# Half-row matmuls of a two-layer mixer kernel given all 128 rows of TensorE's array, with zeros in the rows that are not theirs

## The chip, the core and the metric

The kernel runs on one core of one Trainium2 chip. The metric is the device time of one execution in microseconds (us), median of several runs. TensorE's array has 128 rows (the contraction dimension) and 128 columns. An operand that lies on 64 partitions uses 64 of the rows, and the profile then writes a matmul as 64\*128. Operands are fp32, or fp32r, a form of fp32 that TensorE takes in one pass; a plain fp32 matmul appears in the trace as two records, one for each pass.

## What is computed

Two layers (DEPTH = 2) over 512 tokens, 256 of context and 256 latent, with 1024 features. A layer is a half-step of SwiGLU feed-forward, a mixer, and a second half-step. The mixer has three branches whose gated outputs are summed. In short, from the reference:

```
q, k = heads of differential attention: 4 heads, 2 maps m of 64 features each
s  = einsum('bqhmd,bkhmd->bhmqk', q, k);  pr = softmax(s)
y  = (pr[:, :, 0] - lam * pr[:, :, 1]) @ v
mLSTM, 4 heads of 64:   s = einsum('bhtd,bhsd->bhts', qb, kb) * exp(dlog - mt)
RWKV-7, per direction:  w_raw = w0[d] + tanh(p[wl]) @ w2[d]     (64 x 512)
                        a     = sigmoid(a0[d] + p[al] @ a2[d])  (64 x 512)
```

All three have a contraction over 64 values: a map of an attention head, an mLSTM head, a direction's low-rank matrix. In the last layer context queries are not needed.

## The kernel before

Every dense product is made exact in fp32 by splitting each operand in a leading part hi and a remainder lo, and adding three fp32r matmuls (hi by hi, hi by lo, lo by hi). A unit is 128 x 1024 weights: SP loads it into `raw`, ScalarE casts it to `hi` (L140), VectorE subtracts to get `lo` (L144), and TensorE runs 24 matmuls of 128\*128 on it (`fm_tile`, or `tm_group` with 256 columns each). These are the rows named d and m. All matmuls go through the helper `mm` (L102), all transposes through `tr` (L105).

Within a mixer, the work of two kinds is mixed. The RWKV-7 branch goes through four tiles t of 128 channels; each has elementwise work with small matmuls (`rwkv_stage1`, `rwkv_stage2`), a triangular solve (`rwkv_solve`: 64 matmuls of 32\*32, sG and sB, behind 31 steps on VectorE) and a chain over eight chunks (`rwkv_chain`: X, U, S, Y, of 64\*64 and 128\*64). It runs under `tc.high_priority()`. Everything else (`mixers`: attention, then mLSTM, then the merge) is a generator that yields after each step with an estimate of its time; the table BUDGET says how much of it is put behind each RWKV-7 tile, and the rest follows at the end. The order on each engine is what the framework's scheduler makes of the program, by priority and by its own costs, so an edit at one place can move instructions elsewhere.

The matmuls that the change touches:

- **Attention scores**, aS. `attn_rot` makes q and k of a head, feature-major, in two tiles qkT [128, 512]: map 0 on partitions 0 to 63, map 1 on 64 to 127. `attn_head` takes the 64 rows of one map for each matmul, fp32.
- **mLSTM scores**, mS. Two heads share a tile mqk, one on each half of the partitions; the head's 64 rows are taken, fp32.
- **Low-rank low parts**, loral. The hi part lorah carries the direction's matrix twice, so that x with hi on one half and lo on the other is a 128-row matmul (lw, la from lorah). The remainder loral [128, 2, 128] is used on the direction's 64 rows only, fp32r.
- **Gate-row transposes**, gT. The mLSTM gates have 64 rows gi and 64 rows Fc; each is transposed in four blocks against a 64 x 64 identity.

The same 64\*128 form remains, untouched, in A (`rwkv_stage2`). 

Of the kernel before, what the change touches and what calls it, by code (L numbers as in the profile page):

```python
# [9 lines left out]
F32 = mybir.dt.float32  # L10
# [25 lines left out]
# columns of the packed per-partition parameters  # L36
# [3 lines left out]
# columns of the packed constants  # L40
# [10 lines left out]
# per layer: gate tiles after each attention and mLSTM head; other work (in us of TensorE) before and after  # L51
# the columns of each next recurrent tile
# [24 lines left out]
SPLIT = 16  # L77

class Halves:
    """a unit's 1024 columns in two tiles"""
# [9 lines left out]
class Builder:  # L92
# [36 lines left out]
    def unit(self, spec):  # L129
        """hi and lo parts of a unit; exact together"""  # L130
# [16 lines left out]
    def unit_early(self, spec):  # L147
        """a unit in room that the feed-forward part doesn't need yet"""
        raw = self.fp.tile([P, 1024], F32, name="araw", tag="araw", bufs=4)
        self.unit_load(raw, spec)  # L150
        r = []
        for i, tag in enumerate(("uh", "ul")):
            r.append(Halves([self.fp.tile([P, 1, NT], F32R, name=tag, tag=tag, bufs=14) for _ in range(2)]))
        for n in range(2):
            c = slice(n * NT, (n + 1) * NT)
            self.split(r[0][:, c], r[1][:, c], raw[:, c])
        return r
# [4 lines left out]
    def fm_tile(self, spec, lo=0, h=None, ps=None):  # L162
        """one feature-major tile of 128 columns: PSUM [128 cols, tokens]"""
        hi, lw = self.unit(spec)
        return self.fm_mm(hi, lw, range(KT), slice(lo, NT), h or self.h, ps=ps)
# [15 lines left out]
    def fm_first(self, units, pss, parts):  # L181
        """the first tiles after a norm: every feature block goes to all of them as soon as it is there"""
# [10 lines left out]
    def split(self, hi, lo, src):  # L193
        """exact split of src: hi carries the leading half of the significand"""
# [3 lines left out]
    def rsqrt(self, out, in_, eps, scale=1.0):  # L198
        """out = 1/sqrt(scale*in + eps)"""
# [8 lines left out]
    def ada_first(self, i, j):  # L208
        """block j of modulation vector i (0 shift, 1 scale) of the first norm, on TensorE"""
# [18 lines left out]
    def ada_first_shift(self, j):  # L228
        """the shift on VectorE"""
# [13 lines left out]
    def load_c(self, after=lambda: None):  # L243
        """silu of the two condition vectors on every partition"""
# [23 lines left out]
    def ada_steps(self):  # L268
        """the others on VectorE: one block of 128 outputs at a time"""
# [27 lines left out]
    def sqrt_ahead(self):  # L297
        """has ScalarE's table for the square roots of the next norm loaded before they are due"""
# [4 lines left out]
    def sumsq(self, k, c):  # L303
        """adds the squares of x_k to the running sum of these tokens"""
# [9 lines left out]
    def norm_stats(self, parts):  # L314
        """1 / rms of these tokens on every partition, in PSUM"""
# [16 lines left out]
    def norm_apply(self, l, i, k, psr, parts):  # L332
        """feature block k of the modulated norm, split into hi and lo"""
# [12 lines left out]
    def norm_mod(self, l, i, parts):  # L346
        """norm and modulation of these tokens"""
# [5 lines left out]
    def x_update(self, l, gi, k, ps, c):  # L353
        """x_k += 0.5 * gate * ps"""
# [12 lines left out]
    def ffn(self, l, which, lo, ready, after):  # L367
        """ready: the PSUM tiles of the first gate and up tiles;
        after: token ranges with what to do when x has its final value there"""
# [60 lines left out]
    def conv(self, out, ps, w, lo=0):  # L430
        """out = centred 3-tap convolution of ps; w: three [128,1] taps"""
# [11 lines left out]
    def attn_prep(self):  # L443
# [21 lines left out]
        self.qg, self.nl, self.subw = qg, nl, sub  # L465

    def tm_group(self, cols, consume, t0=0):
        """token-major product with 256 columns (cols: (c0, width) ranges): PSUM [128 tokens, 256]
        for each of the token tiles from t0 on"""
# [19 lines left out]
    def attn_qk(self, h):  # L489
        """raw q and k of a head, token-major (token tile, q or k), and the sums of their squares"""  # L490
# [14 lines left out]
    def attn_qk_pair(self, hp):  # L505
        """the same for two heads without the context's q: slots k0 k1 q2 k2 q3 k3 of the token tiles"""
# [32 lines left out]
    def attn_rot(self, qkr, ss):  # L539
        """normalised and rotated q and k of a head, feature-major"""  # L540
# [29 lines left out]
        for w in range(2):  # L570
# [4 lines left out]
            o = a.tile([P, NT], F32, name="qkT", tag="qkT", bufs=4)  # L575
            nc.scalar.copy(o[:, t0 * P :], pt[:, t0 * P :])
# [3 lines left out]
    def attn_head(self, hp, h, qT, kT, v):  # L580
# [3 lines left out]
        for i in range(lo // P, 4):  # L584
# [4 lines left out]
            for m in range(2):  # L589
                pS = self.psm("aS")  # L590
                r = slice(64 * m, 64 * m + 64)
                self.mm(pS[:, : nk * P], qT[r, i * P : (i + 1) * P], kT[r, : nk * P], True, True)
# [52 lines left out]
    def mlstm_steps(self):  # L645
# [4 lines left out]
        def qk(c0, ti, lo):  # L650
# [5 lines left out]
            o = a.tile([P, NT], F32, name="mqk", tag="mqk", bufs=4)  # L656
            nc.vector.scalar_tensor_tensor(o[:, lo:], th[:, lo:], 1.0, z[:, lo:], op0=ALU.add, op1=ALU.mult)
            return o

        q, k = [], []  # L660
# [3 lines left out]
        for i in range(2):  # L664
            k.append(qk(O_MK + P * i, 2 + i, 0))
            yield 5
        # gates: rows 0-3 i fwd, 32-35 i bwd, 64-67 f fwd, 96-99 f bwd (others zero)
        pg = self.fm_tile([("w_gate", l, kk * P, 0, P) for kk in range(KT)])
        gb = pv[:, PV_GB : PV_GB + 1]
        gi = a.tile([64, NT], F32, name="gi", tag="P00", bufs=1)  # L670
# [24 lines left out]
        # m = F + G; em = exp(-m); nG = -G, its hi part on the first half of the partitions, lo on the other  # L695
        nc.vector.tensor_tensor(Fc, Fc, G, op=ALU.add)
# [7 lines left out]
        for t in range(4):  # L704
            self.tr(pt[:, t * 64 : t * 64 + 64], gi[:, t * P : (t + 1) * P], 64)
        for t in range(4):
            self.tr(pt[:, 256 + t * 64 : 256 + t * 64 + 64], Fc[:, t * P : (t + 1) * P], 64)
        used = lambda x: x.rearrange("p (t d r) -> p (t d) r", t=4, d=2)[:, :, 0:4]
        nc.scalar.copy(ac.rearrange("p t (d r) -> p (t d) r", d=2), used(pt[:, :256]))
        nc.scalar.activation(em.rearrange("p t (d r) -> p (t d) r", d=2), used(pt[:, 256:]), AF.Exp, scale=-1.0)  # L710
# [5 lines left out]
        for h in range(4):  # L716
            if h % 2 == 0:
# [9 lines left out]
                yield 10  # L727
            ps = self.fm_tile(self.blocks("w_in", l, O_MO + h * P), lo)
            tho = a.tile([P, NT], F32, name="tho", tag="tho", bufs=1)
            nc.scalar.activation(tho[:, lo:], ps[:, lo:], AF.Tanh, scale=0.5)  # L730
            r = slice(64 * (h % 2), 64 * (h % 2) + 64)
            qt, kt = q[h // 2], k[h // 2]
            # s-block j: scores against the query tokens it can reach
# [9 lines left out]
            for j in range(4):  # L743
                s0 = max(lo, 0 if j < 2 else CTX)
                pS = self.psm("mS")
                self.mm(pS[:, s0:], kt[r, j * P : (j + 1) * P], qt[r, s0:], True, True)
                for d in range(2):
                    # reachable query blocks
# [66 lines left out]
    def rwkv_small(self):  # L815
# [6 lines left out]
        # hi and lo parts of a direction on the two halves of the partitions  # L822
# [4 lines left out]
        for src, dst in ((tw, self.tw), (pa, self.ta)):  # L827
            for d in range(2):
                r, o = slice(64 * d, 64 * d + 64), slice(64 - 64 * d, 128 - 64 * d)
                nc.scalar.copy(dst[r, d], src[r])  # L830
                nc.vector.tensor_tensor(dst[o, d], src[r], dst[r, d].bitcast(F32), op=ALU.subtract)
        self.vpad = a.tile([P, 128 + NT], F32, name="vpad", tag="vpad", bufs=1)
# [22 lines left out]
    def rwkv_cols(self, t):  # L855
# [12 lines left out]
        ll = a.tile([P, 2, P], F32R, name="loral", tag="loral", bufs=1)  # L868
        nc.scalar.copy(lh, lw)
        for d in range(2):  # L870
            r = slice(64 * d, 64 * d + 64)
            nc.vector.tensor_tensor(ll[r], lw[r, d::2], lh[r, d::2].bitcast(F32), op=ALU.subtract)
# [9 lines left out]
    def rwkv_stage1(self, t, r, k, v, lw, g2):  # L882
        """everything that is elementwise over (channel, token)"""
# [5 lines left out]
        # normalised keys  # L889
# [5 lines left out]
        # 1 / max(norm, 1e-12)  # L895
# [7 lines left out]
        for d in range(2):  # L903
            rows = slice(64 * d, 64 * d + 64)

            def lora(name, i, x):
                ps = self.pss(name)
                self.mm(ps, lw[0][:, 2 * i + d], x[:, d], True, False)
                self.mm(ps, lw[1][rows, i], x[rows, d], False, True)
# [36 lines left out]
    def rwkv_stage2(self, t, r, k, v, g2, kk, eC, dirs):  # L946
# [6 lines left out]
        # token-major v and the u of each chunk: head 0 has v on partitions 0-63 and u on 64-127,  # L953
        # head 1 the other way round. Token window w is tokens 64w-64 .. 64w+64
# [46 lines left out]
        # bonus  # L1001
# [7 lines left out]
    def rwkv_solve(self, t, Zf):  # L1009
        """Bt[(h, s), (d, c), t] = transpose of (I - A)^-1, A strictly triangular in (t, s)"""  # L1010
        nc, a = self.nc, self.a2
        Bt = self.Bts[t % 2]
        # Zf[(h, s), (d, c), t]: the diagonal blocks first
# [7 lines left out]
        # backward units: transpose within the block so that every unit is strictly lower in (row, col)  # L1021
# [6 lines left out]
        # two sets of columns in turn, so that VectorE always has an independent instruction  # L1028
# [13 lines left out]
        # back: R[row, u, col]  # L1042
# [6 lines left out]
        # forward units: Rn = T (t, s), Rt = T^T; backward units: Rn = T^T, Rt = T  # L1049
# [5 lines left out]
        # off-diagonal blocks  # L1055
# [107 lines left out]
    def rwkv_post(self, t, y, g2, bon, dst=None):  # L1163
        """group norm, bonus, gate"""
# [25 lines left out]
    def gate(self, b, o):  # L1190
        """tanh(g / 2) of a gate tile"""
# [17 lines left out]
    def gates_ahead(self, n):  # L1209
        """gate tiles computed before the merge, parked in DRAM"""  # L1210
# [8 lines left out]
    def branch_in(self, b, ks):  # L1219
        """hi and lo parts of a branch's output"""  # L1220
# [17 lines left out]
    def merge_steps(self):  # L1238
        """z = sum over branches of 2 sigmoid(g) * (y @ P_b), without the recurrent branch yet"""
# [21 lines left out]
    def merge_last(self, y):  # L1261
        """the recurrent branch; z as hi and lo parts in the place of h"""
# [15 lines left out]
    def mixers(self, es):  # L1278
        """attention, mLSTM and the merge of their outputs, in steps"""
# [8 lines left out]
    def build(self):  # L1288
# [76 lines left out]
        for l in range(DEPTH):  # L1365
# [52 lines left out]
            # in this order: the gates are in use longer than what lies under x  # L1418
# [38 lines left out]
def constants():  # L1457
# [7 lines left out]
    # exponents of the masked part of a diagonal block; the others are at most 0  # L1465
# [102 lines left out]
```

## Time and profile before

| | |
|---|---|
| median of 3 runs | 2867.44 us |
| lowest and highest of them | 2856.05 and 2876.06 us |
| span of the profiled execution, first to last instruction | 2880.2 us |
| TensorE (PE) busy | 2784.9 us, 97% |
| weight loads (PEld) busy | 2280.8 us, 79% |
| VectorE (DVE), ScalarE (ACT), GpSimd (POOL) busy | 65%, 40%, 8% |
| mean granted TensorE clock | 0.962 of full |

What the profiled execution took outside its span is not shown; the span alone lies above the highest of the three runs. The profile's busy time of PE contains time in which a matmul only drains or waits for its weights, because matmuls overlap and their ends are modelled: how long one really holds the engine is read from the distance between starts. [...]

### The profile page before, as it was taken

What the parts mean: (1) busy time and instruction counts of PE and PEld (TensorE: products, weight loads), DVE (VectorE), ACT (ScalarE), POOL (GpSimd) and SP (SyncE); (2) the same over time, 40 slices, a digit from 0 to 9 for tenths busy, and PEclk for the clock granted to TensorE, in tenths of its full rate; (3) what the DMA queues carried; (4) which work ended last, traced back from release to release, by engine and by line L of the source; (5) the groups of instructions that cost most, each with busy time, mean ns of one, the idle gap of its engine ahead of it and who ended that gap; (6) DMA issues with size and microseconds to landing.
All of it is one profiled execution on the core that took longest, in us unless ns stands there. A gap on an engine that the chain in (4) does not pass through costs nothing.

```text
span 2880.2 us, 43519 instructions
## 1 busy us (share of the span) xinstructions
PE 2784.9 (97%) x17198; PEld 2280.8 (79%) x17198; DVE 1862.6 (65%) x3611; ACT 1146.1 (40%) x1955; POOL 236.5 (8%) x330
## 2 busy tenths in 40 slices
PE   7999999999999999999999999999999899998999
PEld 5888887668676677688888888888878677878999
DVE  7999368474593663589995443333877677746654
ACT  3322244443553543343222332222554546444543
POOL 0000002111110200200000000000212121112000
PEclk9999999799997999999999999999989899989999
DMA  7777322111121222666773232222221121226454
GB/s 264 237 238 227 100 94 68 34 63 39 59 75 41 70 74 80 225 205 221 237 240 109 88 102 96 95 95 74 98 78 57 61 65 57 92 92 214 162 183 147
DMA packets 102432, 349.65 MB, mean 121 GB/s; under 512 B 13362, under 2 KB 17842, under 8 KB 101972
## 3 DMA queue, kind: packets, MB, share of 16 engines
q1 hardware_dynamic: 91872, 315.10, 33.5%
q0 software_dynamic: 9024, 31.60, 3.3%
q8 instruction: 135, 2.21, 0.3%
q14 instruction: 69, 0.57, 0.1%
q10 hardware_dynamic: 1332, 0.18, 0.0%
HBM read 327.82 MB, written 19.01 MB: 120 GB/s over the span
## 4 chain that ended last, share of the span: by engine, by line
PE 60%; DVE 8%; issue 4%; ACT 3%; DMA 2%; POOL 1%; DVEq 0%; POOLq 0%; ACTq 0%; SPq 0%
PE d L102 25%; PE m L102 22%; PE Y L102 2%; PE A L102 2%; DVE lo L144 1%; PE X L102 1%; DVE op L1038 1%; DVE T L1041 1%; DMA yin<-yd 1%; DMA raw<-in_ws 1%; PE mo L102 1%; PE aS L102 1%; PE S L102 1%; PE U L1116 1%; ACT hi L140 1%
## 5 line engine op out<-in xcount | busy, mean ns | idle before, releaser
L140 ACT CAST hi<-raw 128x1024 fp32r<-128x1024 f32 x430 | 451.0, 1049 | 1022.0 <-PE m L102 468.0
L144 DVE TENSOR_TENSOR lo<-raw,hi 128x1024 fp32r<-128x1024 f32 (+1 forms) x508 | 544.6, 1076 | 322.7 <-ACT hi L140 315.6
L102 PE MATMUL m<-hh,hi 128*128 128x512 f32 (+1 forms) x1440 | 510.8, 357 | 3.9 <-ACT hh L342 2.5
L102 PE MATMUL m<-hl,hi 128*128 128x512 f32 (+1 forms) x1440 | 513.2, 357 | 0.0
L102 PE MATMUL m<-hh,lo 128*128 128x512 f32 (+1 forms) x1440 | 512.5, 357 | 0.0
L102 PE MATMUL d<-hh,hi 128*128 128x256 f32 (+1 forms) x976 | 357.5, 367 | 4.0 <-DVE x L359 2.7
L102 PE MATMUL d<-hl,hi 128*128 128x256 f32 (+1 forms) x976 | 353.1, 362 | 0.4 <-DVE hl L196 0.4
L102 PE MATMUL d<-hh,lo 128*128 128x256 f32 (+1 forms) x976 | 349.1, 358 | 0.1
L239 DVE SCALAR_TENSOR_TENSOR ajunk<-araw,scb 128x1024 f32<-128x1024 f32 x272 | 332.5, 1222 | 5.1 <-ACT scb L266 0.5
L102 PEld LDWEIGHTS m<-hh,hi 128*128 128x128 f32 x1440 | 272.0, 190 | 45.3 <-ACT hh L342 3.1
L102 PEld LDWEIGHTS m<-hh,lo 128*128 128x128 f32 x1440 | 272.8, 190 | 40.2 <-DVE lo L144 0.2
L102 PEld LDWEIGHTS m<-hl,hi 128*128 128x128 f32 x1440 | 272.8, 190 | 39.9 <-issue 0.2
L102 PE MATMUL d<-ul,hi 128*128 128x512 f32 (+1 forms) x770 | 269.3, 350 | 0.0
L102 PE MATMUL d<-uh,hi 128*128 128x512 f32 (+1 forms) x770 | 268.5, 349 | 0.0
L102 PE MATMUL d<-uh,lo 128*128 128x512 f32 (+1 forms) x770 | 268.3, 349 | 0.0
L102 PEld LDWEIGHTS d<-hh,hi 128*128 128x128 f32 x976 | 191.9, 197 | 37.5 <-issue 8.2
L102 PEld LDWEIGHTS d<-hl,hi 128*128 128x128 f32 x976 | 191.7, 196 | 34.5 <-issue 12.7
L102 PEld LDWEIGHTS d<-hh,lo 128*128 128x128 f32 x976 | 191.9, 197 | 26.3 <-issue 5.1
L102 PEld LDWEIGHTS d<-uh,hi 128*128 128x128 f32 x770 | 145.1, 188 | 20.8
L102 PEld LDWEIGHTS d<-ul,hi 128*128 128x128 f32 x770 | 145.4, 189 | 19.7
L102 PEld LDWEIGHTS d<-uh,lo 128*128 128x128 f32 x770 | 144.9, 188 | 19.9
L102 PE MATMUL d<-lo,hh 128*128 128x256 f32 x480 | 142.9, 298 | 0.0
(357 smaller groups left out, 4268.3 us busy)
## 6 DMA issues: line engine op xcount, KB each, us to landing
raw<-in_ws SPq DMA_DIRECT2D x430, 512.0 KB, 3.4
araw<-in_ws SPq DMA_DIRECT2D x146, 512.0 KB, 4.4
gd<-gth POOLq DMA_DIRECT2D x24, 256.0 KB, 2.5
gth<-gd SPq DMA_DIRECT2D x24, 256.0 KB, 2.9
xd<-x POOLq DMA_DIRECT2D x2, 2048.0 KB, 7.9
gd<-gth POOLq DMA_DIRECT2D x24, 128.0 KB, 2.0
gth<-gd SPq DMA_DIRECT2D x24, 128.0 KB, 3.3
yin<-yd POOLq DMA_DIRECT2D x11, 256.0 KB, 4.6
```

Of the source, the lines that this page charges most:

```text
L102: self.nc.tensor.matmul(out, lhsT=lhsT, rhs=rhs, start=start, stop=stop)
L140: self.nc.scalar.copy(hi, raw)
L144: self.nc.vector.tensor_tensor(lo[:, c], raw[:, c], hi[:, c].bitcast(F32), op=ALU.subtract)
L239: self.nc.vector.scalar_tensor_tensor(junk, raw, 1.0, self.scb[:, st], op0=ALU.mult, op1=ALU.mult, accum_out=self.mods[l][:, s, k, st : st ...
L1038: nc.vector.tensor_tensor(w, A[:, i + 1 :, i : i + 1].broadcast_to(w.shape), T[:, i : i + 1, c].broadcast_to(w.shape), op=ALU.mult)
L1041: nc.vector.tensor_tensor(t, t, w, op=ALU.add)
L1116: self.nc.tensor.matmul(pu[ur, d * 64 : d * 64 + 64], lhsT=Bt[hr, 8 * d + cs[d]], rhs=X[hr, d], start=True, stop=True, tile_position=(hr.s ...
```

## The change

Each of the four kinds of matmul gets operands on all 128 partitions, one of them with zeros in the half that does not belong to it.

- q of a head goes to a tile qz [128, 2, 512], zeroed once per layer: its map-0 rows to plane 0, its map-1 rows to plane 1, by two 64-row copies in place of one copy. There is one such tile (QZ = (1, 1)) for all heads of a layer; before, qkT had four buffers. k stays in qkT with two buffers.
- k of mLSTM goes to mkz [128, 2, 512] in the same way, by two 64-row instructions. As there is one mkz, the k of heads 2 and 3 is computed later: behind the values of that pair, not ahead of the gates.
- loral gets four planes, zeroed once per layer.
- gi and F + G lie on the two halves of one tile gf, and four 128 x 128 transposes take the place of eight.

The comments and docstrings that the diff also removes are left out here.

```diff
+QZ = (1, 1)
...
+        self.qz, self.nq = [a.tile([P, 2, NT], F32, name="qz", tag=f"qz{i}", bufs=1) for i in range(QZ[l])], 0
+        for t in self.qz:
+            nc.gpsimd.memset(t, 0.0)
...
-            o = a.tile([P, NT], F32, name="qkT", tag="qkT", bufs=4)
-            nc.scalar.copy(o[:, t0 * P :], pt[:, t0 * P :])
+            if w == 0:
+
+                o = self.qz[self.nq % QZ[l]]
+                self.nq += 1
+                for m in range(2):
+                    mr = slice(64 * m, 64 * m + 64)
+                    nc.scalar.copy(o[mr, m, t0 * P :], pt[mr, t0 * P :])
+            else:
+                o = a.tile([P, NT], F32, name="qkT", tag="qkT", bufs=2)
+                nc.scalar.copy(o, pt)
...
-                r = slice(64 * m, 64 * m + 64)
-                self.mm(pS[:, : nk * P], qT[r, i * P : (i + 1) * P], kT[r, : nk * P], True, True)
+                self.mm(pS[:, : nk * P], qT[:, m, i * P : (i + 1) * P], kT[:, : nk * P], True, True)
...
-            o = a.tile([P, NT], F32, name="mqk", tag="mqk", bufs=4)
-            nc.vector.scalar_tensor_tensor(o[:, lo:], th[:, lo:], 1.0, z[:, lo:], op0=ALU.add, op1=ALU.mult)
+            if ti < 2:
+                o = a.tile([P, NT], F32, name="mqk", tag="mqk", bufs=2)
+                nc.vector.scalar_tensor_tensor(o[:, lo:], th[:, lo:], 1.0, z[:, lo:], op0=ALU.add, op1=ALU.mult)
+                return o
+
+            o = kz
+            for n in range(2):
+                r = slice(64 * n, 64 * n + 64)
+                nc.vector.scalar_tensor_tensor(o[r, n], th[r], 1.0, z[r], op0=ALU.add, op1=ALU.mult)
             return o
...
-        for i in range(2):
-            k.append(qk(O_MK + P * i, 2 + i, 0))
-            yield 5
+        kz = a.tile([P, 2, NT], F32, name="mkz", tag="mkz", bufs=1)
+        nc.gpsimd.memset(kz, 0.0)
+        qk(O_MK, 2, 0)
+        yield 5
...
-        gi = a.tile([64, NT], F32, name="gi", tag="P00", bufs=1)
+        gf = a.tile([P, NT], F32, name="gf", tag="P00", bufs=1)
+        gi = gf[0:64]
...
-        nc.vector.tensor_tensor(Fc, Fc, G, op=ALU.add)
+        nc.vector.tensor_tensor(gf[64:128], Fc, G, op=ALU.add)
...
-            self.tr(pt[:, t * 64 : t * 64 + 64], gi[:, t * P : (t + 1) * P], 64)
-        for t in range(4):
-            self.tr(pt[:, 256 + t * 64 : 256 + t * 64 + 64], Fc[:, t * P : (t + 1) * P], 64)
+            self.tr(pt[:, t * P : (t + 1) * P], gf[:, t * P : (t + 1) * P])
...
+                if h:
+                    qk(O_MK + P, 3, 0)
+                    yield 5
...
-                self.mm(pS[:, s0:], kt[r, j * P : (j + 1) * P], qt[r, s0:], True, True)
+                self.mm(pS[:, s0:], kz[:, h % 2, j * P : (j + 1) * P], qt[:, s0:], True, True)
...
+        self.ll = a.tile([P, 4, P], F32R, name="loral", tag="loral", bufs=1)
+        nc.gpsimd.memset(self.ll.bitcast(F32), 0.0)
...
-            nc.vector.tensor_tensor(ll[r], lw[r, d::2], lh[r, d::2].bitcast(F32), op=ALU.subtract)
+            nc.vector.tensor_tensor(ll[r, d::2], lw[r, d::2], lh[r, d::2].bitcast(F32), op=ALU.subtract)
...
-                self.mm(ps, lw[1][rows, i], x[rows, d], False, True)
+                self.mm(ps, lw[1][:, 2 * i + d], x[:, d], False, True)
```

The change also moves instructions. On TensorE around the first solve of layer 0, the program before has (aS the scores of head 0, amT and ay the transposes and the product behind them, sG and sB the solve):

```order
L105 MATMUL amT<-idt,ae 128x128 x2
L102 MATMUL aS<-qkT 128x512
L102 MATMUL ay<-am,av 128x128
L1067 MATMUL sG<-Rn,Z 32x32 x8
L102 MATMUL ay<-am,av 128x128
L102 MATMUL aS<-qkT 128x512
L1067 MATMUL sG<-Rt,Z 32x32 x8
```

and the program after has

```order
L1090 MATMUL sG<-Rn,Z 32x32 x8
L106 MATMUL amT<-idt,ae 128x128 x2
L103 MATMUL aS<-qkT,qz 128x512
L1090 MATMUL sG<-Rt,Z 32x32 x8
L1090 MATMUL sG<-Rn,Z 32x32 x8
L1090 MATMUL sG<-Rt,Z 32x32 x8
L103 MATMUL ay<-am,av 128x128 x2
L103 MATMUL aS<-qkT,qz 128x512
L1103 MATMUL sB<-Rt,Gs 32x32 x8
```

The two scores went from ahead of most of the solve's matmuls to places among them. On TensorE behind the third solve of layer 0, the program before has (nG and mS belong to mLSTM head 0, X and U to the RWKV-7 chain, d to dense work):

```order
L102 MATMUL X<-UV,Ma 64x64 x4
L102 MATMUL nG<-GS,pick 128x512
L102 MATMUL mS<-mqk 128x512
L102 MATMUL d<-hh,hi 128x512
L102 MATMUL d<-hl,hi 128x512
L102 MATMUL d<-hh,lo 128x512
L1116 MATMUL U<-X,Bt 64x64
```

and the program after has, inside the solve,

```order
L1090 MATMUL sG<-Rn,Z 32x32 x8
L103 MATMUL d<-hh,hi 128x512
L103 MATMUL d<-hl,hi 128x512
L103 MATMUL mS<-mqk,mkz 128x512
L1090 MATMUL sG<-Rt,Z 32x32 x8
```

The head's scores start earlier, since one dense tile (the second k) no longer stands ahead of them, and three of the four leave the chain behind the solve.

## Rows read from the trace of the kernel before

**Rows 1.** The page: busy time, and granted clock in 40 equal slices (tenths).

```profile
PE 2784.9 (97%) x17198; PEld 2280.8 (79%) x17198; DVE 1862.6 (65%) x3611; ACT 1146.1 (40%) x1955; POOL 236.5 (8%) x330
...
PEclk9999999799997999999999999999989899989999
```

**Rows 2.** What PE waited for in the two mixers, 420 to 1222, then 2000 to 2690.

```profile
PE m L102 <- ACT yh L195: 4.3, 3, 2.4
...
PE d L102 <- DVE r L439: 0.2, 1, 0.2
...
PE qkT L105 <- DVE qkr L568: 7.9, 2, 4.5
...
PE A L102 <- DVE Mr L983: 0.7, 2, 0.3
```

**Rows 3.** Groups of PE by form: records, busy us, mean ns, idle before.

```profile
L102 PE MATMUL aS<-qkT 64*128 64x512 f32 x64 | 35.0, 712 | 0.0
...
L102 PE MATMUL mS<-mqk 64*128 64x256 f32 x48 | 17.9, 472 | 0.4 <-DVE marg L774 0.4
...
L102 PE MATMUL mS<-mqk 64*128 64x512 f32 x16 | 10.9, 765 | 0.0
...
L102 PE MATMUL la<-tas,loral 64*128 64x512 f32 x16 | 8.0, 498 | 0.0
...
L102 PE MATMUL aS<-qkT 64*128 64x256 f32 x32 | 7.6, 428 | 0.0
```

**Rows 4.** Timeline of PE around a low-rank product: start, duration, instruction.

```profile
438.26 0.39 PE L102 MATMUL d<-hh,hi 128*128 128x512 f32 x1
438.49 0.39 PE L102 MATMUL la<-tas,lorah 128*128 128x512 f32 x1
438.81 0.50 PE L102 MATMUL la<-tas,loral 64*128 64x512 f32 x1
439.24 0.50 PE L102 MATMUL d<-hl,hi 128*128 128x512 f32 x1
439.58 0.39 PE L102 MATMUL d<-hh,lo 128*128 128x512 f32 x1
```

**Rows 5.** Timeline of PE around a 128-row fp32 matmul of 512 columns.

```profile
830.75 1.02 PE L102 MATMUL bon<-bon,cst 128*128 128x512 f32 x2
831.21 0.80 PE L102 MATMUL d<-hh,hi 128*128 128x512 f32 x1
831.85 0.40 PE L102 MATMUL d<-hl,hi 128*128 128x512 f32 x1
```

**Rows 6.** Timeline of PE around both maps of an attention score, layer 1.

```profile
2250.12 0.28 PE L102 MATMUL d<-hh,lo 128*128 128x256 f32 x1
2250.24 0.28 PE L102 MATMUL d<-hh,hi 128*128 128x256 f32 x1
2250.45 1.13 PE L102 MATMUL aS<-qkT 64*128 64x512 f32 x4
2251.51 0.38 PE L102 MATMUL d<-hl,hi 128*128 128x256 f32 x1
2251.73 0.28 PE L102 MATMUL d<-hh,lo 128*128 128x256 f32 x1
```

**Rows 7.** Windows: us, busy (instructions) of PE, PEld, DVE, ACT, POOL; clock, DMA, GB/s.

```profile
512.60:543.40 30.80, 30.80 (x207) 18.89 (x207) 8.42 (x18) 12.69 (x29) 1.06 (x3) 0.50 0.08 27
543.40:871.00 327.60, 312.04 (x2129) 235.45 (x2128) 215.23 (x460) 156.88 (x281) 50.51 (x60) 0.98 0.17 57
871.00:908.60 37.60, 37.60 (x259) 24.16 (x259) 9.43 (x30) 13.07 (x40) 0.78 (x2) 0.50 0.07 22
```

**Rows 8.** PE on the scores alone, in these stretches: aS, then mS.

```profile
512.60:543.40 30.80, 6.03 (x6) 1.31 (x6) 2.06 (x3) 2.33 (x6) 0.50 0.08 27
...
871.00:908.60 37.60, 6.58 (x8) 1.99 (x8) 3.68 (x9) 0.50 0.07 22
```

**Rows 9.** Groups of ACT, POOL and DVE nearest to what is added.

```profile
L576 ACT COPY qkT<-qkT 128x512 f32<-128x512 f32 x12 | 6.6, 587 | 8.7 <-PE qkT L105 8.7
...
L853 POOL MEMSET Bt<- 128x1024 f32 x2 | 1.9, 972 | 0.0
...
L657 DVE SCALAR_TENSOR_TENSOR mqk<-mt,mz 128x512 f32<-128x512 f32 x6 | 4.1, 686 | 0.0
```

More of the change, by code (lines that the diff above doesn't have):

```diff
@@ L655, in qk @@
             nc.scalar.activation(th[:, lo:], z[:, lo:], AF.Tanh, scale=0.5)
-            o = a.tile([P, NT], F32, name="mqk", tag="mqk", bufs=4)
-            nc.vector.scalar_tensor_tensor(o[:, lo:], th[:, lo:], 1.0, z[:, lo:], op0=ALU.add, op1=ALU.mult)
+            if ti < 2:
[6 more added lines that the diff above has]
+                nc.vector.scalar_tensor_tensor(o[r, n], th[r], 1.0, z[r], op0=ALU.add, op1=ALU.mult)
             return o
-        q, k = [], []
+        q = []
         for i in range(2):
@@ L704, in mlstm_steps @@
         for t in range(4):
-            self.tr(pt[:, t * 64 : t * 64 + 64], gi[:, t * P : (t + 1) * P], 64)
-        for t in range(4):
-            self.tr(pt[:, 256 + t * 64 : 256 + t * 64 + 64], Fc[:, t * P : (t + 1) * P], 64)
-        used = lambda x: x.rearrange("p (t d r) -> p (t d) r", t=4, d=2)[:, :, 0:4]
-        nc.scalar.copy(ac.rearrange("p t (d r) -> p (t d) r", d=2), used(pt[:, :256]))
-        nc.scalar.activation(em.rearrange("p t (d r) -> p (t d) r", d=2), used(pt[:, 256:]), AF.Exp, scale=-1.0)
+            self.tr(pt[:, t * P : (t + 1) * P], gf[:, t * P : (t + 1) * P])
+        used = lambda i: pt.rearrange("p (t i d r) -> p t i d r", t=4, i=2, d=2)[:, :, i, :, 0:4]
+        as4 = lambda x: x.rearrange("p t (d r) -> p t d r", d=2)
+        nc.scalar.copy(as4(ac), used(0))
+        nc.scalar.activation(as4(em), used(1), AF.Exp, scale=-1.0)
         yield 5
@@ L730, in mlstm_steps @@
             nc.scalar.activation(tho[:, lo:], ps[:, lo:], AF.Tanh, scale=0.5)
-            r = slice(64 * (h % 2), 64 * (h % 2) + 64)
-            qt, kt = q[h // 2], k[h // 2]
+            qt = q[h // 2]
             nG = []
@@ L867, in rwkv_cols @@
         lh = a.tile([P, 4, P], F32R, name="lorah", tag="lorah", bufs=1)
-        ll = a.tile([P, 2, P], F32R, name="loral", tag="loral", bufs=1)
+        ll = self.ll
         nc.scalar.copy(lh, lw)
@@ L903, in rwkv_stage1 @@
         for d in range(2):
-            rows = slice(64 * d, 64 * d + 64)
             def lora(name, i, x):
```

## The prediction

> **What bounds the kernel now.** I read the page's busy shares first, then what TensorE waits for, then the forms of its matmuls, and last the distance between starts around the matmuls that change. TensorE is busy for 97% of the span, the others for 65%, 40% and 8% [rows 1]. Busy time of TensorE can hide waits, so the list of its waits in the two mixers matters more: 17 kinds in each, from 4.3 us down to 0.2 and from 7.9 down to 0.7, which add up to 33.6 and 34.5 us [rows 2]. That is 68 of the 1,492 us in those stretches, under 5%. So TensorE sets the pace, and a microsecond that it no longer needs is nearly a microsecond of the kernel. The reader should see that the matmuls concerned are few: their groups hold some 80 us of modelled busy time [rows 3] (low-rank lw, not shown, is as large as la). No speed-up of their streams could do much. What can is what they cost their neighbours.
>
> **The cost of changing form.** Around one low-rank product [rows 4] the starts are 438.26, 438.49, 438.81, 439.24 and 439.58. Between plain 128-row neighbours the distance is 0.23. The last 128-row matmul ahead of the 64-row one takes 0.32, the 64-row one 0.43, the one behind it 0.34: 1.09 in place of 0.69, so 0.40 us for going to 64 rows and back, 0.20 for each change of form. [...] The columns streamed stay the same after the change, and rows of zeros cost nothing in time: a 128-row fp32 matmul of 512 columns goes from 830.75 to 831.85 with one dense matmul of 0.23 behind it [rows 5], so 0.87 for its two passes, while the 64-row pass streams no faster.
>
> How many changes of form go away is a matter of order. I went through both programs' order on TensorE and counted each place where a matmul has other rows or columns than the one ahead: 1,203 before, 1,036 after, 167 fewer. That is less than two for each of the 48 aS, 32 mS and 32 loral, since some stand together, and some stand beside X, U, S, Y or sG, where a 128-row matmul changes form just as a 64-row one does. 167 by 0.20 is 33.4 us. In stretches at the lower clock a change costs more; I leave that out.
>
> **What is given up.** The two maps of an attention score lie on different halves of the rows, and where they stand side by side they run at once. In [rows 6] everything from 2250.24 to 2251.73 is 1.49 us; taking off two dense matmuls of 256 columns (0.12 each, by the distance 2250.12 to 2250.24) and 0.40 for the two changes of form leaves 0.85, the time of two passes of 512 columns, though four were issued. With 128 rows the two maps go one after the other: 0.87 more for a pair of 512 columns, 0.43 for one of 256. The order before has such pairs at nine places, four of 512 (all in layer 1) and five of 256: 4 by 0.87 plus 5 by 0.43 is 5.6 us. That leaves 27.8 us.
>
> The trace thus shows two halves sharing the array. [...]
>
> **Where the gain lands.** Some of these drains fall where TensorE waits for something anyway, so of the 27.8 us I take nine tenths, 25. What is late next is still TensorE.
>
> **The clock.** [...] Both low stretches begin at a solve, whose matmuls use 32 rows, and go on into the chain of 64-row matmuls. In the first the aS hold 6.0 us, in the second the mS 6.6 us [rows 8]. If what the array does counts by rows, these matmuls count for half now and in full later, and the clock should rise earlier. If both stretches vanished, half of 68.4 us would be saved, 34.2; if the rows make no difference, nothing; and the moved order could also cost some. The solve and the chain are unchanged and keep most of what pulls the clock down, so I take a quarter, 8 us. [...]
>
> **What is added.** ScalarE copies q in two 64-row pieces: 8 more instructions of up to 587 ns, 4.7 us in all, on an engine busy 40%. VectorE writes k of mLSTM in two pieces: 4 more of up to 686 ns, 2.7 us. GpSimd clears qz and mkz in each layer, 4 by 972 ns, and loral, half as large, twice: 4.9 us on an engine busy 8% [rows 9]. All lie beside dense matmuls; without that cover they would cost up to 12 us. I put down 1. The single qz makes ScalarE's copy for the next head wait for the last score of this head, with weight casts queued behind it, which TensorE needs; but the transposes that feed the copy already stand behind those scores on TensorE, so nothing is waited for twice. The second k of mLSTM moves by one dense tile and its GpSimd clear stands ahead of use by far. gT now waits for both gate rows at once rather than twice; I count no gain and no loss.
>
> **The sum.** Minus 25, minus 8, plus 1: 32 us less. The profiled span, 2880.2, is already 4 us above the slowest run shown, so the difference is taken from the median of the runs: 2867.4 minus 32 is 2835 us, 1.1% less. The three runs spread over 20 us, 0.7%, and about 1%, 28.7 us, is what a measurement of this kernel can tell from no change.
>
> **The rivals.**
>
> First, the forecast: changes of form saved, the clock a little better, 2835. The counted changes and the measured 0.20 speak for it. Its own range is 2822 to 2850. Chance 0.45.
>
> Second, the clock ignores rows. Then only minus 25 plus 1 remain: 2843. For it: TensorE is recorded busy throughout the low stretches, so busy time alone doesn't explain them, but neither does the trace show rows to be the reason; solve and chain may suffice. Chance 0.22.
>
> Third, the clock gains more: both low stretches halve, 17 us, and 2867.4 minus 25 minus 17 plus 1 is 2826. For it: one of the two stretches begins among 64-row scores. Against it: their scores move within the solve, and what fills the chain behind it is other work. Chance 0.14.
>
> Fourth, sharing the array was worth more than the nine pairs. With all 24 pairs lost the gain is 33.4 minus 17.4, 16, and nine tenths of it with the 1 us leave 13: 2854. Against it: the pairs that don't stand side by side in the order can't overlap. Chance 0.11.
>
> Fifth, slower: the clock falls where it did not. The order moved three mS from the chain behind the third solve of layer 0 into that solve; the chain is left with less 128-row work, and there are eight solves with such chains. A further low stretch like the longest, 37.6 us [rows 7], costs half, 18.8. To be 28.7 us slower, the 24 gained must also be eaten: 53 us, some three such stretches more. That point is far, but the scheduler moved much, and a table tuned for the old order may fit less. It would give about 2900. Chance 0.08.
>
> **How the numbers follow.** Faster by over 1% means below 2838.8: two thirds of the forecast (0.30), the third rival (0.14), a quarter of the second (0.06): 0.50. Slower by over 1%: the fifth, 0.08. The rest, 0.42, is within 1%. The range leaves out the fifth rival and the far ends: from 2810, the third rival with all of the 27.8 and a run below the median, up to 2866, the fourth with all 12 us of uncovered additions.
>
> **What would show it.** The forms 64\*128 of aS, mS, loral and gT are gone, and the starts around a low-rank product are 0.23 apart. Pairs of scores in layer 1 take some 0.5 us longer from neighbour to neighbour. Two dense stretches, feed-forward above all, take what they took. The low stretches behind the first and third solve are shorter, or the second rival holds. The prediction is wrong if neighbours of 128-row scores still lie further apart, if TensorE's waits in the mixers grow well beyond 68 us, or if new low stretches appear.

## The result and the profile after

The changed kernel takes 2845.24 us (median of 5, 2834.89 to 2850.73) against 2874.99 for the kernel before in the same comparison: ratio 0.9895, 95% interval 0.9857 to 0.9933. Run again later, it took 2841.09 us, ratio 0.9906 (0.9878 to 0.9934). So it is 1.0% faster: 29 to 30 us by the medians, 27 by the means of either comparison. The forecast was 2835 us and 32 us less. Executions more than 1.5% above the fastest of their kernel are left out of all ratios and means below, so their count can be lower than that behind a median.

The page, to be read beside [rows 1] (share of the span, then the granted clock in 40 slices):

```profile
PE 2717.4 (96%) x17190; PEld 2258.3 (80%) x17190; DVE 1865.2 (66%) x3615; ACT 1147.3 (40%) x1962; POOL 237.4 (8%) x336
...
PEclk9999999999999999999999999999999999999999
```

The profiled execution took 2834.89 us, 2833.1 of them span. VectorE, ScalarE and GpSimd do as much as before; TensorE is recorded busy for 67 us less. Windows around the first and the third solve of layer 0 (us, busy and instructions of PE, PEld, DVE, ACT, POOL, then the granted clock), where [rows 7] had two long stretches at 0.50:

```profile
505.00:547.00 42.00, 41.27 (x394) 28.75 (x393) 24.21 (x55) 25.51 (x55) 7.06 (x10) 0.98 0.10 33
...
849.00:889.00 40.00, 40.00 (x465) 29.79 (x465) 21.46 (x70) 19.50 (x60) 2.61 (x6) 1.00 0.13 41
```

Both stretches are gone: the clock is 0.98 and 1.00. It is not these two alone. From 8 us ahead of each solve's first sB to 32 us behind it, the eight solves held 152 us at 0.50 before (seven of them 10 to 36 each, the fourth none) and hold 20 now; over the whole profiled execution it was 218 us and is 113. A second profile of the changed kernel (e8) has 28 there and 144 in all, and one stretch of 30.7 us from 664.7, just behind the second solve.

In the three long stretches where TensorE's order is the same in both programs (ahead of, between and behind the two mixers), it takes 492.3, 986.1 and 268.3 us before and 492.4, 983.9 and 270.6 now. So the gain lies in the mixers.

TensorE around the same low-rank product as in [rows 4] (start, duration, instruction):

```profile
436.43 0.39 PE L103 MATMUL d<-hh,hi 128*128 128x512 f32 x1
436.66 0.39 PE L103 MATMUL la<-tas,lorah 128*128 128x512 f32 x1
436.89 0.40 PE L103 MATMUL la<-tas,loral 128*128 128x512 f32 x1
437.13 0.39 PE L103 MATMUL d<-hl,hi 128*128 128x512 f32 x1
437.36 0.40 PE L103 MATMUL d<-hh,lo 128*128 128x512 f32 x1
```

From 436.66 to 437.36 it is 0.70 for what took 1.09: the 0.40 is gone here, as forecast. The weight loads show where it was, first before, then after. Before, the load of loral and the one behind it stand open, with the loading idle for 0.35 and 0.25 us ahead of them; now they follow at the pace of the others.

```profile
438.27 0.19 PEld L102 LDWEIGHTS la<-tas,lorah 128*128 128x128 f32 x1
438.81 0.18 PEld L102 LDWEIGHTS la<-tas,loral 64*128 64x128 f32 x1 [0.35 <-issue]
439.24 0.19 PEld L102 LDWEIGHTS d<-hl,hi 128*128 128x128 f32 x1 [0.25 <-issue]
```

```profile
436.66 0.19 PEld L103 LDWEIGHTS la<-tas,loral 128*128 128x128 f32 x1
436.89 0.19 PEld L103 LDWEIGHTS d<-hl,hi 128*128 128x128 f32 x1
```

The forms, beside [rows 3], and the largest waits of the two mixers, beside [rows 2] (first from 420 to 1185, then from 1963 to 2643):

```profile
L103 PE MATMUL aS<-qkT,qz 128*128 128x512 f32 x64 | 33.5, 613 | 0.0
L103 PE MATMUL mS<-mqk,mkz 128*128 128x256 f32 x48 | 13.9, 392 | 0.0
...
L103 PE MATMUL la<-tas,loral 128*128 128x512 f32 x16 | 6.6, 411 | 0.0
```

```profile
PE gv L103 <- ACT gsq L1197: 7.9, 2, 4.4
...
PE gT L106 <- DVE gf L717: 4.3, 1, 4.3
...
PE mS L103 <- DVE mkz L675: 1.8, 1, 1.8
```

```profile
PE qkT L106 <- DVE qkr L572: 7.0, 2, 3.7
PE X L103 <- DVE S L1181: 5.0, 4, 2.2
...
PE gT L106 <- DVE gf L717: 4.4, 1, 4.4
```

All kinds added up, the waits went from 33.8 and 36.6 us to 40.1 and 49.5: 70 to 90. The 64-row forms are gone, but TensorE waits for other engines more often.

What was added, beside [rows 9]:

```profile
L585 ACT COPY qz<-qkT 64x512 f32<-64x512 f32 (+1 forms) x16 | 7.6, 473 | 10.8 <-PE qkT L106 10.7
...
L675 DVE SCALAR_TENSOR_TENSOR mkz<-mt,mz 64x512 f32<-64x512 f32 x8 | 5.5, 686 | 0.6 <-ACT mt L666 0.5
```

### The profile page after: what moved, and what is told of

Read it like the earlier page. It is cut to its first block, busy times and chain, and to the rows that moved or that the text cites. A ratio compares the mean times of both kernels' runs of the same rounds, so it can differ in the third digit from the quotient of the medians.

```text
span 2833.1 us, 43526 instructions
## 1 busy us (share of the span) xinstructions
PE 2717.4 (96%) x17190; PEld 2258.3 (80%) x17190; DVE 1865.2 (66%) x3615; ACT 1147.3 (40%) x1962; POOL 237.4 (8%) x336
## 3 DMA queue, kind: packets, MB, share of 16 engines
q1 hardware_dynamic: 91872, 315.10, 34.1%
## 4 chain that ended last, share of the span: by engine, by line
PE 76%; DVE 10%; issue 7%; ACT 4%; DMA 3%; POOL 1%; ACTq 0%; DVEq 0%; POOLq 0%; SPq 0%
PE m L103 31%; PE d L103 31%; PE Y L103 3%; PE A L103 2%; DVE lo L145 2%; PE X L103 1%; DVE op L1061 1%; DVE T L1064 1%; DMA yin<-yd 1%; DVE bk L965 1%; PE S L103 1%; PE mo L103 1%; PE U L1139 1%; PE aS L103 1%; ACT hi L141 1%
## 5 line engine op out<-in xcount | busy, mean ns | idle before, releaser
L103 PE MATMUL d<-hh,hi 128*128 128x512 f32 (+1 forms) x976 | 354.2, 363 | 9.3 <-DVE x L360 4.6
L103 PE MATMUL d<-hl,hi 128*128 128x512 f32 (+1 forms) x976 | 347.3, 356 | 0.4 <-DVE hl L197 0.4
L103 PE MATMUL d<-hh,lo 128*128 128x512 f32 (+1 forms) x976 | 345.1, 354 | 1.2 <-DVE lo L145 1.1
L240 DVE SCALAR_TENSOR_TENSOR ajunk<-araw,scb 128x1024 f32<-128x1024 f32 x272 | 332.4, 1222 | 5.0 <-ACT scb L267 0.5
L103 PE MATMUL d<-hi,hh 128*128 128x256 f32 x480 | 143.6, 299 | 0.2 <-ACT sg L874 0.2
```

The source lines that it names most:

```text
L103: self.nc.tensor.matmul(out, lhsT=lhsT, rhs=rhs, start=start, stop=stop)
L240: self.nc.vector.scalar_tensor_tensor(junk, raw, 1.0, self.scb[:, st], op0=ALU.mult, op1=ALU.mult, accum_out=self.mods[l][:, s, k, st : st ...
```

## The experiments

Two theories had to be told apart. By the first the gain is the changes of form that go away, 0.20 us each. By the second it is the clock: the same matmuls on 128 rows keep TensorE's granted clock at 1.00. A third is that the moved order does it.

Two quantities help. Every execution has its span and mean granted clock, and 2 times (1 minus clock) times span is its **low-clock time**: in the profiled executions of the kernel before and the changed one, 218 and 113 us are at 0.50 and all else is at 1.00. Over 178 executions of all kernels a fit with one slope and one constant for each kernel gives 0.387 us more time (within 0.014) for each us of low-clock time, with 2.1 us left unexplained; for one kernel at a time the slope is 0.27 to 0.44. The difference of two constants is the difference **at equal clock**. In the table it is taken against the changed kernel, with its 95% interval.

The runs were made in four comparisons on four chips (e1 to e4; e5 to e7; e8 to e11; e12), each with the kernel before beside it; the first run of the changed kernel stands outside them. The kernel before itself had 195, 204, 184 and 203 us of low-clock time there, and means of 2872.7, 2875.7, 2867.8 and 2875.5 us; at equal clock the four lie within 1 us. So a difference of plain means between two comparisons can hold up to 19 us of low-clock time, 8 us of time, that is neither kernel's own. Where it matters, the difference **beside its own before** is given too: the kernel less the kernel before of its comparison, set against the same for the changed kernel in e8.

| kernel | median, us | ratio to before (95%) | low-clock, mean of executions | at equal clock |
|---|---|---|---|---|
| before | 2870.0 to 2876.3 in four comparisons | | 197 of 76 | +9.0 ± 1.5 |
| changed, both comparisons | 2845.24, 2841.09 | 0.9895, 0.9906 | 139 of 11 | 0 |
| e1 all on 64 rows | 2875.89 | 1.0009 (0.9979 to 1.0040) | 190 of 9 | +15.0 ± 2.0 |
| e2 loral on 64 | 2843.12 | 0.9861 (0.9817 to 0.9905) | 121 of 4 | +5.0 ± 2.4 |
| e3 aS on 64 | 2876.01 | 0.9986 (0.9957 to 1.0014) | 203 of 10 | +5.5 ± 2.0 |
| e4 mS on 64 | 2856.97 | 0.9926 (0.9897 to 0.9955) | 151 of 10 | +6.6 ± 1.8 |
| e5 aS of the first head on 64 | 2848.00 | 0.9898 (0.9855 to 0.9941) | 147 of 6 | +2.6 ± 2.1 |
| e6 aS of the other heads on 64 | 2862.89 | 0.9937 (0.9903 to 0.9971) | 169 of 11 | +4.4 ± 1.8 |
| e9 extra matmuls, 64 rows | 2865.02 | 0.9988 (0.9963 to 1.0013) | 144 of 12 | +21.2 ± 1.7 |
| e11 extra matmuls, 128 rows | 2841.77 | 0.9918 (0.9888 to 0.9949) | 113 of 6 | +12.8 ± 2.1 |
| e12 extra matmuls and aS on 64 | 2881.36 | 1.0026 (1.0004 to 1.0049) | 194 of 12 | +18.9 ± 1.9 |
| e7 gT later | 2835.50 | 0.9858 (0.9813 to 0.9904) | 126 of 5 | −1.2 ± 2.2 |
| e10 gT later in layer 1 | 2832.45 | 0.9895 (0.9856 to 0.9933) | 132 of 6 | −2.4 ± 2.1 |

**All three kinds back on 64 rows (e1).** The changed kernel, its buffers, copies and its order on every engine kept; only the rows taken differ:

```diff
-                self.mm(pS[:, : nk * P], qT[:, m, i * P : (i + 1) * P], kT[:, : nk * P], True, True)
+                r = slice(64 * m, 64 * m + 64)
+                self.mm(pS[:, : nk * P], qT[r, m, i * P : (i + 1) * P], kT[r, : nk * P], True, True)
...
-                self.mm(pS[:, s0:], kz[:, h % 2, j * P : (j + 1) * P], qt[:, s0:], True, True)
+                self.mm(pS[:, s0:], kz[r, h % 2, j * P : (j + 1) * P], qt[r, s0:], True, True)
...
-                self.mm(ps, lw[1][:, 2 * i + d], x[:, d], False, True)
+                self.mm(ps, lw[1][r, 2 * i + d], x[r, d], False, True)
```

> The changed kernel with all buffers, copies and the order of every engine as they are; only aS, mS and loral take the owner's 64 rows of the zero-padded tiles again. In that order 147 changes of form come back (1,036 to 1,183), and 8 pairs of scores stand side by side. If changes of form are the gain (0.20 us each) the time rises by 29.4 minus 4.8 for the pairs, 25 us, and the low-clock time stays near 113 us. If the clock is the gain, the low-clock time goes back towards 219 us, which costs up to 53 us more. If the moved order or the second k is the gain, the time stays within 5 us of the changed kernel.

Measured: 2875.89 us, the time of the kernel before. Without the rows, the moved order and the additions together gain nothing: the third theory, the order alone, falls. Whether the rows would gain as much in the old order was not run. Against the changed kernel the loss splits in two: 15.0 us at equal clock, and 51 us more at 0.50 (43 beside its own before), worth 17 to 20. The split hangs on the slope: at the 0.45 that e5 shows below for one stretch, the 15.0 would be some 12.

**One kind at a time (e2, e3, e4).** The low-rank line of that diff alone, the aS lines alone, the mS lines alone.

```diff
+                self.mm(ps, lw[1][r, 2 * i + d], x[r, d], False, True)
```

> The changed kernel with loral alone back on 64 rows, same order. 51 changes of form come back: by their price 10 us slower. These products stand among dense matmuls, far from the low stretches, so by the clock alone the time stays within 3 us and the low-clock time at 113 us.

```diff
+                self.mm(pS[:, : nk * P], qT[r, m, i * P : (i + 1) * P], kT[r, : nk * P], True, True)
```

> The changed kernel with the attention scores aS alone back on 64 rows, same order. 58 changes of form come back, 11.6 us, and 8 pairs run side by side again, 4.8 us: by the price of form 7 us slower. [...]

```diff
+                self.mm(pS[:, s0:], kz[r, h % 2, j * P : (j + 1) * P], qt[r, s0:], True, True)
```

> The changed kernel with the mLSTM scores mS alone back on 64 rows, same order. 38 changes of form come back: by their price 8 us slower. [...]

Measured against the changed kernel, by means of the executions: −2, +30 and +11 us (−6, +26 and +7 beside its own before, each within 10). With loral on 64 rows TensorE pays at the sites what was forecast (e2, to be read beside the rows of the kernel after, above):

```profile
438.01 0.39 PE L103 MATMUL la<-tas,lorah 128*128 128x512 f32 x1
438.33 0.50 PE L103 MATMUL la<-tas,loral 64*128 64x512 f32 x1
438.76 0.50 PE L103 MATMUL d<-hl,hi 128*128 128x512 f32 x1
439.09 0.39 PE L103 MATMUL d<-hh,lo 128*128 128x512 f32 x1
```

From 438.01 to 439.09 it is 1.08, again 0.38 more. Since the order is the same, each site of one trace can be set against the same site of the other: most sites with 128-row neighbours cost 0.36 to 0.40, those with a neighbour of another form on one side (X, U, S, Y) 0.18 to 0.21, and where TensorE waited there anyway some cost nothing or less (2.46 became 1.75 at one). So 0.20 for a change of form holds. The sites at full clock add up to some 7 us for loral and some 6 each for aS and mS. In the time at equal clock 5.0, 5.5 and 6.6 of it arrive. Yet e2 is not slower, since its four executions had 121 us at low clock; its 51 changes of form, among dense matmuls, did not pull the clock down. Most of e3's 30 us is clock: 64 us more of it (56 beside its own before), worth 22 to 25. e4's low-clock time rose by 12 ± 20 only, though its profiled execution had 17 us at 0.50 behind the third solve, where [rows 7] had 37.6.

**A few scores at one place (e5), and all the others (e6).**

```diff
+                r = slice(64 * m, 64 * m + 64) if l == 0 and hp == 0 and h == 0 else slice(0, P)
+                self.mm(pS[:, : nk * P], qT[r, m, i * P : (i + 1) * P], kT[r, : nk * P], True, True)
```

> The changed kernel in which only the 8 scores of the first attention head of layer 0 take 64 rows again, same order on every engine; four of them stand in and behind the first solve. At the price of form that all three kinds together showed at equal clock (15 us for 147 changes and 8 pairs) at most 14 changes come back: under 2 us. [...]

```diff
+                r = slice(64 * m, 64 * m + 64) if not (l == 0 and hp == 0 and h == 0) else slice(0, P)
+                self.mm(pS[:, : nk * P], qT[r, m, i * P : (i + 1) * P], kT[r, : nk * P], True, True)
```

> The complement: the 40 scores of all other heads take 64 rows, those of the first head 128, same order. By the price of form 46 changes and 8 pairs come back, some 5 us over the changed kernel. [...]

The window from 505 to 547, first of e5, then of e6:

```profile
505.00:547.00 42.00, 41.05 (x281) 26.23 (x280) 15.54 (x38) 18.96 (x42) 2.67 (x6) 0.59 0.08 27
```

```profile
505.00:547.00 42.00, 41.16 (x395) 28.26 (x393) 25.63 (x59) 26.58 (x56) 7.25 (x10) 1.00 0.10 33
```

In the profiled executions eight scores decide over this stretch. In all fourteen its clock goes with them: 0.62 before, 0.59 in e1, 0.63 in e3, 0.59 in e5 and 0.84 in e12, where they take 64 rows; 0.96 to 1.00 in the changed kernel, run twice, in e2, e4, e6, e7, e9, e10 and e11, where they take 128. Idle time doesn't sort them: from 8 us ahead of the solve's first sG to 3 us behind its start TensorE idles for 0.3 to 2.4 us in the five, 0.7 to 2.4 in the nine. What TensorE did there, first in the changed kernel, then in e5:

```profile
511.06 0.69 PE L1090 MATMUL sG<-Rn,Z 32*32 32x32 f32 x16 [0.73 <-ACT Rn L1070]
511.68 0.44 PE L106 MATMUL amT<-idt,ae 128*128 128x128 f32 x2
511.95 1.02 PE L103 MATMUL aS<-qkT,qz 128*128 128x512 f32 x2
...
514.89 1.02 PE L103 MATMUL aS<-qkT,qz 128*128 128x512 f32 x2
...
544.03 1.05 PE L103 MATMUL ayr<-ysq,ones 128*128 128x512 f32 x2
```

```profile
508.43 0.69 PE L1091 MATMUL sG<-Rn,Z 32*32 32x32 f32 x16 [0.95 <-ACT Rn L1071]
509.05 0.44 PE L106 MATMUL amT<-idt,ae 128*128 128x128 f32 x2
509.42 1.12 PE L103 MATMUL aS<-qkT,qz 64*128 64x512 f32 x2
...
513.64 2.07 PE L103 MATMUL aS<-qkT,qz 64*128 64x512 f32 x2
...
556.76 1.05 PE L103 MATMUL ayr<-ysq,ones 128*128 128x512 f32 x2
```

The instructions are the same. At 511.0 the clock of e5 falls to 0.50, for 34.1 us, and the second score takes 2.07 us instead of 1.02. From the first sG to ayr e5 takes 48.33 us and the changed kernel 32.97: 15.4 us for 34.1 at 0.50, 0.45 for each, with the few changes of form among them. In the mean over executions this does not show. By the ratios e5 is no slower than the changed kernel; its plain mean is 5.7 us higher, 1 lower beside its own before, and its low-clock time is up by 8 ± 17, where this stretch in every execution would be 34. Either the stretch doesn't come back in every execution or others are shorter in exchange: that stays open.

e6 met its expectation: 4.4 us over the changed kernel at equal clock. It lies 14 us below e3 with most of the changes of form still there, and in the window above its clock is 1.00. Its profile has low stretches in layer 1 instead (23.9 us from 2233.2, 27.3 from 2281.0). They begin close behind scores of the other heads and hold next to none (0.4 us). From 5 us ahead of these scores to 35 behind them, 54 us were low in e6, but only 10 in e3, with the same scores on 64 rows, and 23 in e11, with all on 128. So what holds at the first solve is not shown for every place with scores, and a long low stretch can arise without them, as in e8 behind the second solve.

**More changes of form, or fewer rows (e11, e9, e12).** These three share one order. A matmul of 4 columns, overwritten by the score, goes ahead of each score; on 128 rows in e11, on 64 in e9, and in e12 the score takes 64 rows too.

```diff
+                self.mm(pS[:, :4], qT[:, m, i * P : (i + 1) * P], kT[:, :4], True, True)
```

> The control: the same 48 extra matmuls of 4 columns on all 128 rows, same order on every engine, no change of form added. Against the changed kernel it costs the 48 matmuls and what the scheduler moved, 5 us or so (29 changes of form more from the moved order), with a low-clock time of about 140 us.

```diff
+                self.mm(pS[:, :4], qT[r, m, i * P : (i + 1) * P], kT[r, :4], True, True)
```

> The changed kernel with one more matmul ahead of each of the 48 scores: the same operands, the owner's 64 rows, 4 columns, overwritten by the score itself. It adds 86 changes of form (1,065 to 1,151 in its order), more than the 58 that the scores on 64 rows had, and takes no rows away. Compared with the same kernel with this matmul on 128 rows. If the rows set the clock, the low-clock time stays the same in the two, and the difference is the price of form: 17 us at 0.20 us each, 9 to 12 us at the 0.11 to 0.14 that the runs so far gave at equal clock. If it is the changes of form themselves, or the drains with them, that pull the clock down, the low-clock time is 60 us or more above the other's and the difference 35 us or more.

```diff
+                self.mm(pS[:, :4], qT[r, m, i * P : (i + 1) * P], kT[r, :4], True, True)
+                self.mm(pS[:, : nk * P], qT[r, m, i * P : (i + 1) * P], kT[r, : nk * P], True, True)
```

> The kernel with the extra 4-column matmuls on 64 rows, in which the score behind each of them takes the owner's 64 rows as well; same order on every engine. It has 27 changes of form less than the one with 64-row extras and 128-row scores (1,124 against 1,151), and 7 pairs of scores lie side by side. If changes of form or their drains set the clock, the low-clock time is below that kernel's 144 us and the time 5 to 9 us below its 2,865. If the rows set it, the low-clock time rises to about 200 us, as with the scores on 64 rows alone, and the time lies some 10 us or more above it, though there is less to drain.

From e11 to e9, which stood side by side, 86 changes of form more cost 8.4 ± 2.1 us at equal clock, 0.10 each, and 31 ± 21 us more at 0.50, 12 us: neither none, as the rows alone would have it, nor the 60 of the other theory. From e9 to e12 there are 27 changes less, yet the low-clock time rises by 51 ± 21 us and the time by 17, while at equal clock it falls by 2.3. The two stood in different comparisons; beside its own before it is 32 ± 24 us and 10 ± 9. Here only the rows of the scores differ and the two theories point opposite ways: so the rows weigh on the clock by themselves. Changes of form do too (e9 against e11); which of them weighs more, intervals this wide don't tell. e11's own +12.8 at equal clock is 48 matmuls and an order that the scheduler changed around them; it says nothing of rows.

**The gate transposes later (e7, e10), and the base run.** The block that transposes gf moves behind the values of the first mLSTM head, in both layers (e7) or in layer 1 only (e10):

```diff
+            if h == 0:
+                pt = self.psm("gT")
+                for t in range(4):
+                    self.tr(pt[:, t * P : (t + 1) * P], gf[:, t * P : (t + 1) * P])
...
+            if l and h == 0:
+                ac, em = gate_rows()
```

> The changed kernel with the transposes gT and the two copies behind them written at the first mLSTM head, behind the values, so that TensorE has some dense matmuls more ahead of them. If the waits of gT for gf (4.3 and 4.4 us) and the short falls of the clock behind them are a real cost, both go and the time falls by 5 to 12 us, to some 2,835. If the wait merely moves to another place, it stays within 4 us of the changed kernel.

> The changed kernel with the gate transposes written later in layer 1 only. In layer 0 the wait for gf had turned into one of the solve for Rn (1.0 to 5.8 us); in layer 1 it fell from 4.4 to 1.7 us. If the wait and the fall of the clock behind it are worth what they seem, 3 to 6 us below the changed kernel and no more than 5 us above the version with both moved (2,835); if that version's lead came from chance in the clock, no difference from the changed kernel.

> The changed kernel, unaltered, as the base for the other three on the same chip: 2,845 us, low-clock time about 140 us in the mean of its executions (112 in the profiled one earlier).

The base gave 2841.09 us. e7 and e10 are 6 and 5 us below the changed kernel in the mean (13 ± 12 and 4 ± 9 beside its own before), of which 1.2 and 2.4 at equal clock; the rest is a low-clock time that lies within chance. In e7 the wait of layer 0 only changed its name (gT's 4.3 us are gone, sG's for Rn grew from 1.0 to 5.8). These two have the lowest medians of the study and are at most slightly better than the change itself; the intervals don't part them.

## Why the prediction was right, and where its terms were not

The time was right to 10 us and the gain to 5, but partly by luck: two terms erred in opposite ways. By the means of all executions (2872.9 to 2841.6) it is 31.3 less, in the two comparisons of the changed kernel 27.5 and 27.0:

| step of the prediction | forecast | measured |
|---|---|---|
| changes of form, less the pairs | −25 | −15.0 ± 2.0 (e1 against changed, equal clock) |
| clock | −8 | −19 to −22 (at 0.50 48 ± 15 us less in e8 beside its own before, 58 ± 12 over all executions; by 0.387) |
| additions, moved order, gT | +1 | +6.0 ± 1.4 (e1 against before, equal clock) |

**TensorE bounds the kernel**: right. The freed time came out of the span, though a part of it came back as waits, 70 us before, 80 in e1, 90 after. The prediction's 68 us leave out the shortest waits: its "17 kinds in each" are the longest of 18 and 23. By its own list, waits well beyond 68 us are a sign of being wrong; this sign came up, and the gain held all the same.

**The price of a change of form**, 0.20: right at every kind of site. The term was mis-sized at "I take nine tenths". In e1's order 147 changes and 8 pairs come to 24.6 us; the sites that could be compared at full clock add up to some 19, and 12 to 15 arrive in the time. What the trace shows of the cause is the weight load that stands open, with the loading idle for 0.35 and 0.25 us (above); that a matmul drains there, as the prediction's "these drains" has it, no run shows. At a clock of 0.50 the price is higher: the dense matmul ahead of a change takes 0.56 us and the one behind it 0.59 (kernel before, 882.30 to 882.86 and 883.27 to 883.86), where plain neighbours are 0.43 apart; at 1.00 it is 0.32 and 0.34 against 0.23 [rows 4].

**Pairs given up**: right for 256 columns. Where two maps stand side by side, e3 takes 1.28 us from neighbour to neighbour (492.44 to 493.72) and the changed kernel 1.33 (495.11 to 496.44):

```profile
492.44 0.39 PE L103 MATMUL d<-hh,lo 128*128 128x512 f32 x1
492.76 0.70 PE L103 MATMUL aS<-qkT,qz 64*128 64x256 f32 x4
...
493.72 0.39 PE L103 MATMUL d<-hl,hi 128*128 128x512 f32 x1
```

```profile
495.11 0.40 PE L103 MATMUL d<-hh,lo 128*128 128x512 f32 x1
495.35 1.03 PE L103 MATMUL aS<-qkT,qz 128*128 128x256 f32 x4
...
496.44 0.40 PE L103 MATMUL d<-hl,hi 128*128 128x512 f32 x1
```

That fits two changes of form saved (0.39) and one pair's overlap lost (0.43). The pairs of 512 columns, expected 0.5 us longer, stand beside waits or low clock in one trace or the other and show no clean price.

**The clock**: that the rows of the scores count was right, the size was not. The step that failed is "so I take a quarter": it looked at two stretches of layer 0 and assumed that solve and chain hold the clock down by themselves. Seven of the eight solves had such stretches (152 us, now 20), and at the first, where it was tried, the scores among the solve's 32-row matmuls tip it in the profiled executions. The second rival, that rows make no difference, is refuted by e12 against e9 and by this stretch in fourteen profiles. The recorded busy time doesn't part the two states of this stretch: in the window from 505 to 547 it is 41.3 us at 0.98 (394 instructions, changed kernel) and 41.1 at 0.59 (281, e5).

**Additions**: 1 us was too little. What of the 6 is copies, gT's wait for both rows, or the second k moved, was not separated; gT's waits grew from 3.5 and 3.6 us to 4.3 and 4.4, and moving it later gave back 1.2 ± 2.2 and 2.4 ± 2.1 (e7, e10). mS's wait of 1.8 us for mkz is new.

**The rivals**: the third was nearer on the clock, and the fourth lost too many pairs. No run shows its 17.4 us, all 24 pairs at the price of [rows 5], 16 by 0.87 and 8 by 0.43: nine stood side by side before and 8 in e3, and the one of 256 columns set out above fits 0.43. The fifth's new low stretch did appear in e8 (30.7 us from 664.7, where the kernel before has 13.7 from 662.8), but the low-clock time as a whole fell (197 to 139 us in the mean).

## What to carry to other kernels

Before giving a half-empty matmul all rows, list the stretches at the lower clock and see whether such matmuls stand in them: here the clock was worth at least as much as the changes of form (some 20 us against 15). Price a change of form from starts at one site and multiply by the count in the order, but expect half to two thirds of it in the time. Where executions of one kernel spread, compare them at equal clock: it made differences of 5 us readable in a spread of 30, and kernels from different chips comparable.

## What was not expected of the hardware

Rows that add nothing to the result weigh on the granted clock: from e9 to e12 only they go, and the low-clock time rises by 32 ± 24 us beside its own before. The zeros are in the weights alone; the other operand streams the other half's values through these rows, and zeros on both sides were not run. In the profiled executions eight matmuls of about 1 us or less decide whether 34 us run at a granted clock of 0.50 or 1.00. And nearly all of the spread between executions of one kernel is low-clock time (108 to 177 us for the changed kernel): 0.387 us for each us of it, with 2.1 us left. Why it is 0.387 was not tested. Plain dense neighbours of 512 columns start 0.43 us apart at 0.50 and 0.23 at 1.00 (kernel before, 517.33 to 518.19, and [rows 4]), which would be some 0.46; the one stretch that could be priced from starts, in e5, cost 0.45.
